# Asking for the raw rotary blocks of the first two-map head at the attention's begin

## The chip, the cores and the metric

One core of a Trainium2 chip runs the whole kernel. The metric is the device time of one execution in microseconds. The kernel before took 2370.1 us, the median of three runs (2368.41 to 2372.17). Its engines are TensorE (PE in the profile, with PEld for its weight loads), VectorE (DVE), ScalarE (ACT), GpSimd (POOL) and SyncE (SP). Each has its own queue of instructions and runs it in order. Transfers (DMAs) are issued from the queues of SP, ACT and POOL.

## The reference

Two layers of an encoder run over 512 tokens of width 1024 in float32. Each layer is a half-step feed-forward network, a mixer and a second half-step feed-forward network. The mixer is what the change touches:

```
u = rmsnorm(h);  proj = u @ w_in
qa, ka, va, qb, kb, vb, qc, kc, vc, gl = split(proj)
oa = neighbourhood_attention(qa, ka, va, rpb)            # 8 heads, A
ob = sliding_window_attention(rope(qb), rope(kb), vb, sink)   # 8 heads on 2, B
oc = differential_attention(rope(qc), rope(kc), vc, lam)  # 4 heads, two maps each, C
gates = sigmoid(gl + b_gate)                              # one per branch
merged = sum_n gates[n] * (branch[n] @ w_branch[n])
h = h + rmsnorm(merged @ w_out)

def apply_rope(t, cos, sin):
    t1, t2 = split(t, 2)
    return t * cos + concat(-t2, t1) * sin
```

## The kernel before

Activations lie with the features on the 128 partitions and 512 tokens along the row. A float32 product is made from split operands: a value is taken apart into a high part (on ACT) and the rest (on DVE), and three matmuls add up high by high, high by low and low by high. `mm3` does this in lines 326 to 328, and `dense1` calls it for one output block of 128 features over all the input blocks. Its weights come from DRAM in 512 KB pieces (`fetch`, tile wr, mostly from ACT's queue in this stage) and are split by `ensure` (L224 on ACT, L225 on DVE).

A layer projects first. The project stage computes queries, keys and values of all three branches, and POOL stores many of them to DRAM: split halves (tile part) and the unrotated query and key blocks of branch C (tile raw, eight in a layer, L1405). Then the mixer stage begins. A string, ORDER, lists its units in the order in which the program writes them:

```
qa0 qa1 aa0 gb0 gb1 qa2 aa1 ga0 qa3 aa2 ga1 kb qb0 aa3 ga2 ga3 qb1 ab0 ...
... qb3 ab2 gb6 gb7 qc0 ab3 ga4 ga5 qc1 ac0 ...
```

A unit qa loads what one pair of heads of branch A needs: stacked queries and keys (`restacked`, tile st, two DMAs of 64 rows each, L1783 and L1784), values (`values`, tile x from part, L1760) and the raw relative-position bias (braw, L1729). A unit aa does that pair's attention: scores on TensorE (L1675), the maximum with the bias added (L1678), exponentials on ACT, the reciprocal of the sum (L1692), then in `rest` a transpose (L1706), a split (`split`, L352 and L353) and the product with the values (L1709 and L1710). Units ga, gb and gc are the gates, dense matmuls on TensorE that wait for nothing but weights. A unit kb loads the rotary tables cosR and sinR (`tables_in`, L1943). A unit qc loads one head of branch C: `qkv_c` calls `rope` for its query and its key block. `rope` issues from SP the raw block (x, L1760) and four DMAs of 32 rows that load the same block with its halves swapped (sh, L1768), and then lets DVE multiply x by cosR (L1769), sh by sinR (L1770) and add them (L1771).

The order in which the program writes these units is not the order on the engines. In the mixer, up to its output product, a scheduler places every instruction on its engine's queue, by the order of the program as priority and by its own model of times. It also places the buffers: the tag tx has five slots (x and sh of `rope`), st has fourteen. So DVE's first rotary product of branch C stands in the middle of branch A's second and third pair, and dense matmuls of the gates are spread between the scores and the value products. The DMAs on SP are placed in the same way, and one waits on SP's queue until its buffer and its source are free, and for the landing of earlier transfers; those behind it wait with it. Lines 1760, 1768 to 1771, 1783, 1784 and 1943 are the ones to follow.

Of the kernel before, what the change touches and what calls it, by code (L numbers as in the profile page):

```python
# [39 lines left out]
QA, KA, VA, QB, KB, VB, QC, KC, VC, GL = 0, 4, 8, 12, 16, 17, 18, 22, 26, 30  # L40
# [79 lines left out]
def encoder_kernel(ctx: ExitStack, tc: tile.TileContext, order, xT, wts, cols, rows, rpb, consts, tables, out):  # L120
# [30 lines left out]
    def big(tag, dt=F32, shape=(P, T), name="v"):  # L151
        if tag in BUFS:
            return sb.tile(list(shape), dt, tag=tag, name=nm(name), bufs=BUFS[tag])
        kind, pool = phase[0]
        return pool.tile(list(shape), dt, tag=tag, name=nm(name), bufs=ABUFS[kind][tag])
# [1482 lines left out]
    def raw_of(l, hd):  # L1638
        return bass.AP(rpb.tensor, (l * 8 + hd) * 16 * RPBW, [[RPBW, 8], [1, 16], [1, 8 * RPBW]])
# [77 lines left out]
    def mixer(l, op, made):  # L1717
# [6 lines left out]
        def ask(hd):  # L1724
            if hd < 2:
                raws[hd] = pre[:, 2 + hd, :]
                return
            raw = raws[hd] = big("g", name="braw")
            nc.sync.dma_start(raw, raw_of(l, hd))  # L1729
# [28 lines left out]
        def load(d, dt=F32, tag="tx"):  # L1758
            x = big(tag, dt, name="x")
            nc.sync.dma_start(f(x), d)  # L1760
            return x

        def rope(c):
            x = load(made[c])
            sh = big("tx", name="sh")
            for q in range(4):
                o = q ^ 1
                nc.sync.dma_start(sh[32 * q : 32 * q + 32], made[c][32 * o : 32 * o + 32])  # L1768
            V.tensor_tensor(out=x, in0=x, in1=turning[0], op=ALU.mult)  # L1769
            V.tensor_tensor(out=sh, in0=sh, in1=turning[1], op=ALU.mult)  # L1770
            V.tensor_tensor(out=x, in0=x, in1=sh, op=ALU.add)  # L1771
            return x

        def restacked(c, both):
            if c in (QA, KA):
                return made[c]
            hi, lo = made[c]
            res = []
            for s in range(2):
                own, pair_ = slice(64 * s, 64 * s + 64), []  # L1780
                for one, two in ((hi, lo), (lo, hi))[: 2 if both else 1]:
                    st = big("st", F32R, name="st")
                    nc.sync.dma_start(f(st)[0:64], one[own])  # L1783
                    nc.sync.dma_start(f(st)[64:128], two[own])  # L1784
                    pair_.append(st)
                res.append((pair_ + [None])[:2])
            return res

        def values(c):
            t = made[c] if c == VA else [load(d, F32R, "st") for d in made[c]]  # L1790
            if c >= VC:
                return t
            v = [x.rearrange("p (b h d) -> p b h d", b=2, h=2) for x in t]
            return lambda j, s: v[j // 2][:, j % 2, s, :]
# [13 lines left out]
        def qkv_a(p):  # L1808
            got = restacked(QA + p, False), restacked(KA + p, True), values(VA + p)
            for s in range(2):  # L1810
                ask(2 * p + s)
            return got

        oa = [sb.tile([P, 4, T], F32R, tag="X", name=nm("oa"), bufs=BUFS["X"]) for _ in range(2)]
# [131 lines left out]
        def qkv_c(hd):  # L1946
            return stacks(rope(QC + hd), False), stacks(rope(KC + hd), True), values(VC + hd)
# [19 lines left out]
        def do(u):  # L1967
            kind, i = u[:2], int(u[2:] or 0)
            if kind == "fc" or kind[0] == "y":
                if kind == "fc" and i >= len(oc) or kind[0] == "y" and (kind[1], 3) not in OT:  # L1970
                    settle()
            if kind == "qa":
                held[u] = qkv_a(i)
            elif kind == "kb":
                tables_in()
                held["kb"] = qkv_b(KB), values(VB)
            elif kind == "qb":
                held[u] = qkv_b(QB + i)
            elif kind == "qc":
                held[u] = qkv_c(i)  # L1980
            elif kind == "aa":
                attn_a(i, *held.pop(f"qa{i}"))
            elif kind == "ab":
                attn_b(i, held.pop(f"qb{i}"), *held["kb"])
            elif kind == "ac":
                attn_c(*held.pop(f"qc{i}"))
            elif kind == "fc":
                finish_c(i)
            elif kind[0] == "g":
                gates("abc".index(kind[1]), i)  # L1990
            elif kind[0] == "y":
                combine("abc".index(kind[1]), kind[1], i)
# [146 lines left out]
```

## Time and profile before

| what | value |
| --- | --- |
| median of three runs | 2370.1 us (2368.41 to 2372.17) |
| the profiled execution's own time | 2370.88 us |
| its span | 2369.1 us |
| TensorE busy | 2342.6 us, 99% |
| VectorE busy | 1892.4 us, 80% |
| ScalarE busy | 1446.8 us, 61% |
| mean granted TensorE clock | 0.996 |

The profile is of one execution. Times in it count from the start of the span. A line of a timeline gives the start, the duration, the engine, the line of the program, the operation with the tile that it writes and those that it reads, and, in brackets, how long the engine was idle before it and what released it. A line of waits gives the waiting operation, what it waited for, the microseconds in all, the number of times and the longest. A line of DMA issues gives the transfer, the queue, the count, the size and the median of the time from issue to landing. The mixer of the first layer begins near 516 us, and that of the second near 1688 us.

### The profile page before, as it was taken

What the parts mean: (1) busy time and instruction counts of PE and PEld (TensorE: products, weight loads), DVE (VectorE), ACT (ScalarE), POOL (GpSimd) and SP (SyncE); (2) the same over time, 40 slices, a digit from 0 to 9 for tenths busy, and PEclk for the clock granted to TensorE, in tenths of its full rate; (3) what the DMA queues carried; (4) which work ended last, traced back from release to release, by engine and by line L of the source; (5) the groups of instructions that cost most, each with busy time, mean ns of one, the idle gap of its engine ahead of it and who ended that gap; (6) DMA issues with size and microseconds to landing.
All of it is one profiled execution on the core that took longest, in us unless ns stands there. A gap on an engine that the chain in (4) does not pass through costs nothing. (4 is left out here: it accounts for less than half of the span.)

```text
span 2369.1 us, 40269 instructions
## 1 busy us (share of the span) xinstructions
PE 2342.6 (99%) x15134; PEld 2109.5 (89%) x15134; DVE 1892.4 (80%) x3082; ACT 1446.8 (61%) x2715; POOL 223.8 (9%) x354
## 2 busy tenths in 40 slices
PE   9999999999999999999999999999999999999998
PEld 8999889997888889998899998889978788899987
DVE  7887988966888668888878878889579876788796
ACT  6555566667777465655655554666687764556563
POOL 0111001110121001110001110011101200011100
PEclk9999999999999999999999999999999999999999
DMA  5566446667565524664525565276774664256642
GB/s 170 162 169 190 154 145 187 207 219 207 168 174 189 167 97 147 166 162 165 175 87 168 162 178 196 102 216 199 222 206 139 195 206 140 97 147 172 190 148 84
DMA packets 138147, 395.16 MB, mean 167 GB/s; under 512 B 19296, under 2 KB 26080, under 8 KB 137440
## 3 DMA queue, kind: packets, MB, share of 16 engines
q1 hardware_dynamic: 102960, 260.37, 35.0%
q0 software_dynamic: 20160, 78.66, 12.4%
q10 hardware_dynamic: 14832, 53.56, 7.4%
q8 instruction: 119, 1.95, 0.3%
q14 instruction: 76, 0.62, 0.1%
HBM read 326.98 MB, written 80.74 MB: 172 GB/s over the span
## 5 line engine op out<-in xcount | busy, mean ns | idle before, releaser
L680 PE MATMUL mm<-X,h 128*128 128x256 f32 x1504 | 268.0, 278 | 1.2 <-DVE v L738 1.2
L680 PEld LDWEIGHTS mm<-X,h 128*128 128x128 f32 x1504 | 228.5, 188 | 2.5 <-DVE v L738 2.0
L225 DVE TENSOR_TENSOR w<-wr,w 128x512 fp32r<-128x512 f32 x264 | 178.9, 685 | 56.2 <-ACT w L224 55.2
L224 ACT ACTIVATE w<-wr 128x512 fp32r<-128x512 f32 x264 | 162.5, 627 | 96.4 <-PE mm L328 40.8
L326 PE MATMUL mm<-X,w 128*128 128x512 f32 (+1 forms) x570 | 218.3, 383 | 1.8 <-ACT X L553 1.8
L328 PE MATMUL mm<-X,w 128*128 128x512 f32 (+1 forms) x570 | 216.4, 380 | 0.8 <-DVE w L225 0.8
L327 PE MATMUL mm<-X,w 128*128 128x512 f32 (+1 forms) x570 | 216.2, 379 | 0.8 <-DVE X L554 0.7
L680 PE MATMUL mm<-ht,h 128*128 128x256 f32 x752 | 210.1, 279 | 0.0
L680 PE MATMUL mm<-ht,l 128*128 128x256 f32 x752 | 210.1, 279 | 0.0
L680 PE MATMUL mm<-lt,h 128*128 128x256 f32 x752 | 209.4, 278 | 0.0
L680 PE MATMUL mx<-ht,h 128*128 128x256 f32 x752 | 208.3, 277 | 0.6 <-ACT v L724 0.6
L680 PE MATMUL mm<-X,l 128*128 128x256 f32 x752 | 208.2, 277 | 0.0
L680 PE MATMUL mx<-ht,l 128*128 128x256 f32 x752 | 208.1, 277 | 0.0
L680 PE MATMUL mx<-lt,h 128*128 128x256 f32 x752 | 207.9, 277 | 0.0
L630 DVE TENSOR_TENSOR l<-wr,h 128x1024 fp32r<-128x1024 f32 x94 | 114.9, 1222 | 65.7 <-PE mm L680 65.7
L662 ACT ACTIVATE h<-wr 128x1024 fp32r<-128x1024 f32 x94 | 99.9, 1062 | 78.7 <-PE mx L680 55.5
L680 PE MATMUL at<-X,w 128*128 128x256 f32 x1128 | 144.2, 277 | 0.0
L680 PEld LDWEIGHTS mx<-ht,h 128*128 128x128 f32 x752 | 141.2, 188 | 1.4 <-ACT v L724 1.4
L680 PEld LDWEIGHTS mm<-ht,l 128*128 128x128 f32 x752 | 141.7, 188 | 0.1
L680 PEld LDWEIGHTS mm<-ht,h 128*128 128x128 f32 x752 | 141.7, 188 | 0.0
L680 PEld LDWEIGHTS mm<-lt,h 128*128 128x128 f32 x752 | 141.7, 188 | 0.0
L680 PEld LDWEIGHTS mx<-ht,l 128*128 128x128 f32 x752 | 141.2, 188 | 0.2 <-DVE l L640 0.2
(458 smaller groups left out, 6802.4 us busy)
## 6 DMA issues: line engine op xcount, KB each, us to landing
wr<-in_wts_dram SPq DMA_DIRECT2D x273, 512.0 KB, 4.6
wr<-in_wts_dram ACTq DMA_DIRECT2D x102, 512.0 KB, 4.1
sum<-in_wts_dram POOLq DMA_DIRECT2D x64, 512.0 KB, 5.3
st<-part SPq DMA_DIRECT2D x120, 128.0 KB, 5.1
ap<-in_wts_dram SPq DMA_DIRECT2D x20, 512.0 KB, 5.6
a<-kept SPq DMA_DIRECT2D x32, 256.0 KB, 6.3
ap<-sum SPq DMA_DIRECT2D x16, 512.0 KB, 4.3
x<-part SPq DMA_DIRECT2D x32, 256.0 KB, 3.8
```

The lines of the kernel that those rows point to most:

```text
L224: A.activation(hi, raw, AF.Copy)
L225: V.tensor_tensor(out=lo, in0=raw, in1=f(hi), op=ALU.subtract)
L326: PE.matmul(acc, w[0], x[0], start=start, stop=False)
L327: PE.matmul(acc, w[0], x[1], start=False, stop=False)
L328: PE.matmul(acc, w[1], x[0], start=False, stop=stop)
L630: V.tensor_tensor(out=w["l1"], in0=self.raws[g][0], in1=f(w["h1"]), op=ALU.subtract)
L662: A.activation(self.W[g]["h24"], self.raws[g][1], AF.Copy)
L680: PE.matmul(acc, ws[i], xs[j], start=start and k == m == 0, stop=stop and k == n - 1 and m == 2, skip_group_check=True,)
```

## The change

A new function `begun(c)` holds the five DMAs that `rope` used to issue itself. `qkv_a(0)`, the loads of branch A's first pair, now calls it for QC and KC, the query and key blocks of branch C's first head, after its own loads in the program. `rope` takes those two from a dictionary and issues the DMAs itself for the other three heads. Both layers have the change. Lines behind it move: in the listings below L1769, L1770 and L1771 become L1775, L1776 and L1777, L1783 and L1784 become L1789 and L1790, and L1943 becomes L1952.

```diff
--- before.py
+++ after.py
@@ -1760,12 +1760,18 @@
             nc.sync.dma_start(f(x), d)
             return x
 
-        def rope(c):
+        def begun(c):
             x = load(made[c])
             sh = big("tx", name="sh")
             for q in range(4):
                 o = q ^ 1
                 nc.sync.dma_start(sh[32 * q : 32 * q + 32], made[c][32 * o : 32 * o + 32])
+            return x, sh
+
+        raws_c = {}
+
+        def rope(c):
+            x, sh = raws_c.pop(c, None) or begun(c)
             V.tensor_tensor(out=x, in0=x, in1=turning[0], op=ALU.mult)
             V.tensor_tensor(out=sh, in0=sh, in1=turning[1], op=ALU.mult)
             V.tensor_tensor(out=x, in0=x, in1=sh, op=ALU.add)
@@ -1809,6 +1815,9 @@
             got = restacked(QA + p, False), restacked(KA + p, True), values(VA + p)
             for s in range(2):
                 ask(2 * p + s)
+            if p == 0:
+                for c in (QC, KC):
+                    raws_c[c] = begun(c)
             return got
 
         oa = [sb.tile([P, 4, T], F32R, tag="X", name=nm("oa"), bufs=BUFS["X"]) for _ in range(2)]
```

The scheduler places everything anew. Three places of the first layer show it; the second layer has the same pattern. The first is SP's queue where the mixer begins, and where the tables stand. In the kernel before, x_7488 is the raw query block, and its swapped pieces are sh_7490:

```order
L211 DMA wr_5748<-in_wts_dram 128x1024
L1783 DMA st_5920<-part_4051 64x512
L1784 DMA st_5920<-part_4053 64x512
...
L1729 DMA braw_6147<-in_rpb_dram 128x1x512
L1729 DMA braw_6149<-in_rpb_dram 128x1x512
L1943 DMA cosR_6548<-in_tables_dram 128x512
L1943 DMA sinR_6550<-in_tables_dram 128x512
L1760 DMA x_7488<-raw_5146 128x512
...
L1729 DMA braw_6359<-in_rpb_dram 128x1x512
L1729 DMA braw_6361<-in_rpb_dram 128x1x512
L1768 DMA sh_7490<-raw_5146 32x512 x4
```

In the changed kernel x_5920 and sh_5922 are of the query block, x_5927 and sh_5929 of the key block:

```order
L211 DMA wr_5748<-in_wts_dram 128x1024
L1760 DMA x_5920<-raw_5146 128x512
L1768 DMA sh_5922<-raw_5146 32x512 x4
L1760 DMA x_5927<-raw_5151 128x512
L1768 DMA sh_5929<-raw_5151 32x512 x4
L1789 DMA st_5934<-part_4051 64x512
L1790 DMA st_5934<-part_4053 64x512
...
L1729 DMA braw_6161<-in_rpb_dram 128x1x512
L1729 DMA braw_6163<-in_rpb_dram 128x1x512
L1952 DMA cosR_6562<-in_tables_dram 128x512
L1952 DMA sinR_6564<-in_tables_dram 128x512
L1760 DMA x_6157<-part_4631 128x512
L1760 DMA x_6159<-part_4633 128x512
```

The ten DMAs moved from behind the tables and further back to a place ahead of the first st; the tables kept their place among the others.

The second place is DVE's queue around the first rotary product. Before:

```order
L1678 ISA s_6235,nmx_6234<-mx_6248,bedge_6228 128x256
L1678 ISA nmx_6234 128x1
L225 TENSOR_TENSOR w_6762<-wr_6760,w_6762 128x512
L1769 TENSOR_TENSOR x_7488<-x_7488,cosR_6548 128x512
L1692 RECIPROCAL l_6252<-l_6252 128x4
L353 TENSOR_TENSOR lo_6267<-at_6263,hi_6266 128x256
L1744 TENSOR_TENSOR bedge_6364<-braw_6147,pre_5225 128x256
L353 TENSOR_TENSOR lo_6276<-at_6272,hi_6275 128x256
L1744 TENSOR_TENSOR bmid_6365<-braw_6147,pre_5225 128x256
```

In the changed kernel:

```order
L1678 ISA s_6249,nmx_6248<-mx_6262,bedge_6242 128x256
L1678 ISA nmx_6248 128x1
L1775 TENSOR_TENSOR x_5920<-x_5920,cosR_6562 128x512
L1776 TENSOR_TENSOR sh_5922<-sh_5922,sinR_6564 128x512
L1775 TENSOR_TENSOR x_5927<-x_5927,cosR_6562 128x512
L1777 TENSOR_TENSOR x_5920<-x_5920,sh_5922 128x512
L1692 RECIPROCAL l_6266<-l_6266 128x4
L353 TENSOR_TENSOR lo_6281<-at_6277,hi_6280 128x256
L1776 TENSOR_TENSOR sh_5929<-sh_5929,sinR_6564 128x512
L1777 TENSOR_TENSOR x_5927<-x_5927,sh_5929 128x512
L353 TENSOR_TENSOR lo_6290<-at_6286,hi_6289 128x256
```

Before, one rotary operation stood ahead of the reciprocal and of L353, and the other five further back. Now four stand ahead of the reciprocal and two behind the first L353.

The third place is TensorE's queue at the first scores of branch A's second pair (mx from st). Before:

```order
L328 MATMUL mm_6088<-X_3648,w_6069 128x512
L1710 MATMUL o_6011<-lo_6025,early_3957 128x256
L1675 MATMUL mx_6160<-st_5926,st_5920 128x256
L1709 MATMUL o_6011<-hi_6033,early_3957 128x256
L1675 MATMUL mx_6160<-st_5929,st_5920 128x256
L1675 MATMUL mx_6164<-st_5926,st_5920 128x256
L1675 MATMUL mx_6164<-st_5929,st_5920 128x256
L1706 MATMUL at_6187<-cons,s_5984 128x128 x2
L326 MATMUL mm_6302<-X_3646,w_6091 128x512
L1710 MATMUL o_6011<-lo_6034,early_3957 128x256
```

In the changed kernel:

```order
L327 MATMUL mm_6316<-X_3647,w_6105 128x512
L328 MATMUL mm_6316<-X_3646,w_6105 128x512
L326 MATMUL mm_6316<-X_3648,w_6120 128x512
L327 MATMUL mm_6316<-X_3649,w_6120 128x512
L328 MATMUL mm_6316<-X_3648,w_6120 128x512
L1675 MATMUL mx_6174<-st_5940,st_5934 128x256
L1675 MATMUL mx_6178<-st_5940,st_5934 128x256
L1709 MATMUL o_6200<-hi_6204,early_3957 128x2x128
L1710 MATMUL o_6200<-lo_6205,early_3957 128x2x128
...
L328 MATMUL mm_6316<-X_3648,w_6120 128x512
L326 MATMUL mm_6316<-X_3648,w_6120 128x512
L1675 MATMUL mx_6174<-st_5943,st_5934 128x256
L1675 MATMUL mx_6178<-st_5943,st_5934 128x256
L327 MATMUL mm_6316<-X_3649,w_6120 128x512
L1709 MATMUL o_6200<-hi_6222,early_3957 128x256
```

The first two of those scores moved behind fifteen more dense gate matmuls, the next two behind nineteen. Further on, 103 dense matmuls of the mixer stood ahead of the second half of these scores before, and 137 do now; ahead of the pair's first product with its values (the first L1710 that reads a loaded x) it was 123 and is 157. When branch B's first scores begin both kernels have 260.

## The prediction

> **What bounds the kernel now.** I read the page's busy table and the waits of TensorE first, then the timeline of PE, DVE and SP around the one large wait, and last the busy time by stage.
>
> ```profile
> PE 2342.6 (99%) x15134; PEld 2109.5 (89%) x15134; DVE 1892.4 (80%) x3082; ACT 1446.8 (61%) x2715; POOL 223.8 (9%) x354
> ...
> PE o L1710 <- DVE lo L353: 6.9, 2, 3.7
> ```
>
> TensorE is busy 99% of the span, so a change that leaves its instructions alone can win only its idle time and whatever lowers its clock. The largest idle entry is 6.9 us in two waits, one per layer, of the value matmul L1710 for DVE's L353. This is the first layer's:
>
> ```profile
> 553.45 0.29 PE L1709 MATMUL o<-hi,x 128*128 128x256 f32 x1
> 553.57 0.39 PE L327 MATMUL mm<-X,w 128*128 128x512 f32 x1
> 553.80 0.40 PE L328 MATMUL mm<-X,w 128*128 128x512 f32 x1
> 557.87 0.58 PE L1710 MATMUL o<-lo,x 128*128 128x256 f32 x1 [3.67 <-DVE lo L353]
> 558.53 0.78 PE L326 MATMUL mm<-X,w 128*128 128x512 f32 x1
> 563.36 0.40 PE L328 MATMUL mm<-X,w 128*128 128x512 f32 x1
> ```
> ```profile
> 550.44 0.68 DVE L225 TENSOR_TENSOR w<-wr,w 128x512 fp32r<-128x512 f32 x1
> 556.73 0.69 DVE L1769 TENSOR_TENSOR x<-x,cosR 128x512 f32<-128x512 f32 x1 [5.60 <-DMA x<-raw]
> 557.34 0.17 DVE L1692 RECIPROCAL l<-l 128x4 f32<-128x4 f32 x1
> 557.43 0.39 DVE L353 TENSOR_TENSOR lo<-at,hi 128x256 fp32r<-128x256 f32 x1
> ```
> ```profile
> 1729.85 0.39 PE L1710 MATMUL o<-lo,x 128*128 128x256 f32 x1 [3.21 <-DVE lo L353]
> 1730.80 0.63 PE L328 MATMUL mm<-X,w 128*128 128x512 f32 x1
> 1733.79 0.55 PE L326 MATMUL mm<-X,w 128*128 128x512 f32 x1
> ```
>
> DVE is idle for 5.60 us in front of the first rotary product, which waits for the raw query block; the split L353 that TensorE needs stands behind it in DVE's queue and has nothing to do with the rotary. From the start of that product to TensorE's restart it is 557.87 − 556.73 = 1.14 us. TensorE ran dry at 557.87 − 3.67 = 554.20, so DVE may come to the product as late as 554.20 − 1.14 = 553.06 before TensorE suffers; it was ready at 551.05 (550.44 + 0.61, the step from 556.73 to 557.34). Its slack is 2.0 us.
>
> The idle time has a tail:
>
> ```profile
> 544.00:552.00 8.00, 8.00 (x46) 6.90 (x46) 6.39 (x28) 6.45 (x20) 0.00 (x0) 1.00 0.92 238
> 552.00:556.00 4.00, 2.20 (x10) 1.37 (x9) 0.00 (x0) 1.30 (x6) 0.00 (x0) 1.00 1.06 278
> 556.00:560.00 4.00, 2.13 (x7) 1.84 (x8) 1.88 (x6) 2.46 (x7) 0.00 (x0) 0.56 0.92 217
> 560.00:564.00 4.00, 4.00 (x13) 3.15 (x12) 1.12 (x4) 0.97 (x4) 0.00 (x0) 0.58 0.88 208
> 564.00:590.00 26.00, 25.53 (x156) 21.98 (x155) 23.77 (x80) 25.00 (x74) 0.54 (x1) 1.00 0.60 174
> 590.00:605.00 15.00, 15.00 (x84) 12.62 (x84) 10.83 (x35) 10.42 (x31) 0.62 (x1) 1.00 0.72 213
> ```
>
> The columns are the stretch, its length, the busy time of PE, PEld, DVE, ACT and POOL, then TensorE's granted clock and the DMA share. After the idle the clock is 0.56 and 0.58. From 558.53 to 563.36 there are eleven steps of dense matmuls in 4.83 us; at the 0.23 us of 553.57 to 553.80 they would take 2.53, so 2.3 us are lost. In the second layer seven steps take 2.99 us instead of 1.61: 1.4 lost. The two waits together cost 6.9 + 2.3 + 1.4 = 10.6 us. That bounds what this change can win.
>
> A shorter wait has no such tail:
>
> ```profile
> 11.55 0.38 PE L326 MATMUL mx<-X,w 128*128 128x256 f32 x1 [2.09 <-ACT w L224]
> ...
> 8.00:12.00 4.00, 1.91 (x15) 1.71 (x15) 2.54 (x7) 2.34 (x7) 0.00 (x0) 1.00 1.01 386
> 12.00:16.00 4.00, 4.00 (x36) 4.00 (x35) 3.97 (x9) 3.81 (x10) 0.00 (x0) 1.00 0.79 265
> ```
>
> Idle of 2.09 us left the clock at 1.00, 3.21 us did not. The Trainium skill, "TensorE: Matmul & The Clock Gate", Part 1: The HAM clock gate, says the same with a figure: the clock halves after an idle window of about 3.4 us, and the window runs free, so a wait near that length is halved or not by its phase. By that rule a left-over wait of 1 us costs 1 us and no more, and one a little over 3 us might bring 0 or some 2 us of tail; the sum below needs only the two rows.
>
> **What goes.** The raw query block now lands long before 550, so the 5.60 us on DVE lose the releaser they are put down to. All of the 10.6 us would go if nothing else were late.
>
> **What is late next: the tables.** The products also need cosR and sinR, and these keep their place on SP's queue, behind the ten new issues:
>
> ```profile
> 495.75 1.07 SPq L1784 DMA_DIRECT2D st<-part  x1
> 516.27 0.44 SPq L1783 DMA_DIRECT2D st<-part  x1
> ...
> 546.81 0.45 SPq L1943 DMA_DIRECT2D cosR<-in_tables_dram  x1
> 547.69 0.33 SPq L1943 DMA_DIRECT2D sinR<-in_tables_dram  x1
> 548.06 0.43 SPq L1760 DMA_DIRECT2D x<-raw  x1
> ...
> 561.43 2.30 SPq L1768 DMA_DIRECT2D sh<-raw  x4
> ```
> ```profile
> st<-part SPq DMA_DIRECT2D x10, 128.0 KB, 5.0
> ...
> cosR<-in_tables_dram SPq DMA_DIRECT2D x1, 256.0 KB, 7.4
> ```
>
> Already in the kernel before, cosR landed at 546.81 + 7.4 = 554.2 and sinR at about 555.1, after the 553.06 at which TensorE begins to suffer; the raw block came just behind them. With everything else in place, taking the raw block away would give back only 556.7 − 554.2 = 2.5 us of DVE's wait. So it matters where both sides now stand.
>
> SP's side: one load and its four swapped pieces take 0.43 + 2.30 = 2.73 us of issue, two sets 5.5 us. Low end of the delay to the tables: none, if the ten fit into the 19.5 us in which SP stood between 496.8 and 516.27. High end: 5.5 us. I take the high end, because SP also waits for landings between its issues and the new ten push every later one back by ten places in that sequence. cosR is then issued at 552.3 and sinR at 553.2, landing (7.4 us) at 559.7 and 560.6.
>
> TensorE's and DVE's side: by the printed order, 123 of the mixer's dense gate matmuls (L326 to L328) stand ahead of the stalled L1710 before and 157 after. The 34 more take 34 × 0.23 = 7.8 us, so TensorE runs dry at 554.20 + 7.8 = 562.0, not 554.2. On DVE four rotary operations instead of one now stand ahead of the reciprocal and L353. From sinR's landing there are three operations (0.61 us each) and the 1.14 − 0.61 = 0.53 us to the restart: 2.36 us. The restart is at 560.6 + 2.36 = 563.0: **TensorE waits 1.0 us**, in each layer, at full clock. Ends of this term: 0 (tables undelayed; the three added operations just fit into the 2.0 us of slack) and 2.1 (sinR 1.1 us later, still no tail).
>
> **What the moved matmuls cost where they left.** The 34 dense matmuls were fillers between softmax steps. The order has both kernels level again, at 260 dense matmuls, when the sliding window's scores begin, near 605. In 564 to 590 ACT is busy 25.00 of 26 us: ACT sets the pace there and dense matmuls only fill TensorE.
>
> ```profile
> L225 DVE TENSOR_TENSOR w<-wr,w 128x512 fp32r<-128x512 f32 x264 | 178.9, 685 | 56.2 <-ACT w L224 55.2
> L224 ACT ACTIVATE w<-wr 128x512 fp32r<-128x512 f32 x264 | 162.5, 627 | 96.4 <-PE mm L328 40.8
> ```
>
> With 34 matmuls go three weight splits (a split weight block serves twelve): 3 × 0.627 = 1.9 us of ACT and 2.1 us of DVE. TensorE's work in the stretch falls by 7.8 us, ACT's by 1.9. Behind it, in 590 to 605, ACT has 15 − 10.42 = 4.6 us free. New idle time of TensorE per layer: at most 7.8 − 1.9 = 5.9 us, if nothing of the 4.6 can be used; at least 5.9 − 4.6 = 1.3. I take **1.7 us**, near the low end: in 590 to 605 it is TensorE's fillers (15.00 of 15) that hold ACT back, so softmax work moves up when they are fewer; and five of the six rotary operations of DVE (3.4 us) leave the tight stretch as well.
>
> **What costs nothing.** The rotary's arithmetic is the same six operations. The second pair's stacked blocks stand behind the new loads on SP:
>
> ```profile
> L1675 PE MATMUL mx<-st,st x28: 276/280/365, 531.2 to 568.8; 128*128 128x256 f32 x28
> ```
>
> Issued up to 5.5 us after 516 to 520 and landing 5.0 us later, they are there by about 531; their first use moves from 531.2 behind fifteen dense matmuls, to 534.6. The cover is 3 us; beyond it TensorE would wait by the difference.
>
> **Sum.** −10.6 + 2 × 1.0 + 2 × 1.7 = −5.2 us. The profiled execution took 2370.88 (span 2369.1 and 1.8 around it), 0.8 over the median of the runs: 2365.7 on its own scale, **2364.9** as a median.
>
> **Rivals.**
> *The tables take the raw block's place in full.* sinR lands 2.2 us later than worked out (562.8), TensorE waits 3.2 us again and the clock drops again. For it: the DMA share of 0.92 to 1.06 from 544 to 560, when the tables travel, and 7.4 us for 256 KB. Against it: 0.5 MB of raw loads leave just this stretch. It gives back 10.6 us, and with some shortage of fillers 2370 to 2372: no change that can be told.
> *Slower: TensorE starves in the softmax stretch.* The place is 564 to 605, where 34 fillers are missing. If ACT cannot pull up work, 5.9 us of idle per layer: −10.6 + 2.0 + 11.8 = +3.2, 2373; if the idle comes in pieces of over 3 us the tail of 1.4 to 2.3 is paid again and it is 2376 to 2377. It decides from (10.6 − 2.0) / 2 = 4.3 us per layer on. For it: ACT at 25.00 of 26. Against it: the 4.6 us free behind.
> *All of it is won.* The tables are not delayed, TensorE's later need covers them, and the fillers aren't missed: 2370.1 − 10.6 = 2359.5. For it: 7.8 us of cover against at most 5.5 of delay. Against it: the tight stretch.
>
> **How the numbers follow.** Forecast 0.50, with a range of its own of 2361 to 2368; tables 0.24; starving 0.14; all won 0.12. A difference under 0.2% (4.7 us: 2365.4 to 2374.8) cannot be told from none here. The forecast's range lies 4.4 of its 7 us below 2365.4, so 0.33 of its 0.50 is faster; with all won and a little of the rest, faster is 0.47. Slower by over 0.2% needs the tail in the starving case or both rivals together: 0.13. The rest, 0.40, is the same. The range of 8 in 10 reaches from all won to starving without tail: 2359.3 to 2373.
>
> **What would show it.** In the changed kernel: DVE's idle before the rotary product put down to cosR or sinR (or gone), no longer to x<-raw; L1710's wait under 2.1 us in both layers and the granted clock 1.00 in the 8 us behind it; cosR issued near 552; and in the 40 us after it TensorE idle by 1 to 3 us more per layer, waiting for DVE or ACT. The prediction is wrong if a wait of 3 us or more stands at that L1710 or at the second pair's first scores, if the clock drops elsewhere, or if idle of over 4 us gathers in the softmax stretch.

## The result

The changed kernel takes 2382.6 us (median of six runs, 2380.2 to 2383.5) against 2369.3 us before (six runs). The ratio is 1.0061, with a 95% interval of 1.0050 to 1.0071: 0.6% slower, some 14 us, where 2364.9 was forecast and 2373 was the upper end of the range.

The changed kernel's busy table, and then its waits of TensorE:

```profile
PE 2343.7 (98%) x15134; PEld 2109.4 (89%) x15134; DVE 1896.1 (80%) x3082; ACT 1448.0 (61%) x2715; POOL 222.8 (9%) x354
```
```profile
PE o L1710 <- DVE lo L353: 13.1, 2, 7.1
PE o L1709 <- ACT hi L352: 3.8, 2, 1.9
...
PE mx L1675 <- DVE nmx L1678: 2.1, 2, 1.1
```

The span grew from 2369.1 to 2381.5, by 12.4 us. TensorE's idle time grew from 2369.1 − 2342.6 = 26.5 to 2381.5 − 2343.7 = 37.8, by 11.3; the other 1.1 us are longer busy time. The wait that was to shrink from 6.9 to 2.0 us grew to 13.1, and two new ones stand beside it. It is the same L1710 in both layers. TensorE's timeline of the changed kernel around it:

```profile
562.85 0.40 PE L326 MATMUL mm<-X,w 128*128 128x512 f32 x1
570.32 0.58 PE L1710 MATMUL o<-lo,x 128*128 128x256 f32 x1 [7.07 <-DVE lo L353]
...
1750.62 0.58 PE L1710 MATMUL o<-lo,x 128*128 128x256 f32 x1 [6.07 <-DVE lo L353]
```

and DVE's:

```profile
567.11 0.69 DVE L1775 TENSOR_TENSOR x<-x,cosR 128x512 f32<-128x512 f32 x1 [7.16 <-DMA cosR<-in_tables_dram]
567.97 0.69 DVE L1776 TENSOR_TENSOR sh<-sh,sinR 128x512 f32<-128x512 f32 x1 [0.16 <-DMA sinR<-in_tables_dram]
568.57 0.69 DVE L1775 TENSOR_TENSOR x<-x,cosR 128x512 f32<-128x512 f32 x1
569.18 0.69 DVE L1777 TENSOR_TENSOR x<-x,sh 128x512 f32<-128x512 f32 x1
569.78 0.17 DVE L1692 RECIPROCAL l<-l 128x4 f32<-128x4 f32 x1
569.87 0.39 DVE L353 TENSOR_TENSOR lo<-at,hi 128x256 fp32r<-128x256 f32 x1
```

DVE no longer waits for the raw block. It waits for the tables, which land 13 us later than before: cosR at 567.1 instead of about 554.2. SP's timeline shows how they came to be so late:

```profile
494.94 1.44 SPq L1760 DMA_DIRECT2D x<-raw  x1
507.78 1.73 SPq L1768 DMA_DIRECT2D sh<-raw  x4
510.64 0.34 SPq L1760 DMA_DIRECT2D x<-raw  x1
512.41 10.40 SPq L1768 DMA_DIRECT2D sh<-raw  x4
522.92 0.49 SPq L1789 DMA_DIRECT2D st<-part  x1
...
536.19 0.44 SPq L1790 DMA_DIRECT2D st<-part  x1
...
551.85 0.45 SPq L1789 DMA_DIRECT2D st<-part  x1
...
556.90 0.62 SPq L1952 DMA_DIRECT2D cosR<-in_tables_dram  x1
557.56 0.48 SPq L1952 DMA_DIRECT2D sinR<-in_tables_dram  x1
```

and SP's waits between 480 and 580 name what it stood for:

```profile
SPq L1768 <- PE mx L680: 11.4, 1, 11.4
SPq L1768 <- DMA wr<-in_wts_dram: 10.3, 2, 8.9
...
SPq L1790 <- DMA wr<-in_wts_dram: 6.3, 1, 6.3
SPq L1789 <- DMA wr<-in_wts_dram: 5.2, 1, 5.2
```

In the kernel before, over the same window:

```profile
SPq L1783 <- DMA part<-lo: 19.3, 1, 19.3
...
SPq L1784 <- DMA wr<-in_wts_dram: 10.1, 2, 7.1
```

The first raw block goes out at 494.9. Its swapped pieces wait 11.4 us, until 507.8, for a matmul of the projection (L680). The last pieces of the key block wait 8.9 us for the landing of a weight load. So the ten entries hold the queue from 494.9 to 522.8. Before, the first st block (two entries) had gone out at 495.2, SP had then stood 19.3 us until one of the projection's stores (part) had landed, and the rest followed from 516.3. Now the first st goes out at 522.9, the twelfth of these entries at 536.2 instead of 524.7, and cosR at 556.9 instead of 546.8. From the first of these entries to cosR, SP waits 38.5 us instead of 32.3 by its rows of waits; the other 4 us of the delay are issue time. Then it takes 10.2 us to land (556.9 to 567.1), not 7.4.

By stage of 10 us (columns as in the windows of before: the stretch, its length, PE, PEld, DVE, ACT, POOL, the granted clock, the DMA share):

```profile
560.00:570.00 10.00, 3.24 (x19) 2.46 (x17) 2.73 (x6) 2.50 (x10) 0.00 (x0) 0.91 0.89 216
570.00:580.00 10.00, 9.69 (x44) 8.32 (x45) 7.47 (x23) 6.55 (x18) 0.06 (x1) 0.74 0.51 139
590.00:600.00 10.00, 8.76 (x57) 7.35 (x55) 6.82 (x25) 9.84 (x31) 0.00 (x0) 1.00 0.54 157
```

The largest part of the loss is the one wait with its slowed tail (560 to 580): 6.2 of the 11.3 us of new idle time are the growth of the wait at L1710. A smaller second one lies near 600, where ACT is busy 9.84 of 10 us and TensorE waits for its L352 (3.8 us in both layers).

### The profile page after: what moved, and what is told of

Its sections match the earlier page's. It is cut to its first block, busy times and chain, and to the rows that moved or that the text cites. A ratio compares the mean times of both kernels' runs of the same rounds, so it can differ in the third digit from the quotient of the medians.

```text
span 2381.5 us, 40264 instructions
## 1 busy us (share of the span) xinstructions
PE 2343.7 (98%) x15134; PEld 2109.4 (89%) x15134; DVE 1896.1 (80%) x3082; ACT 1448.0 (61%) x2715; POOL 222.8 (9%) x354
## 3 DMA queue, kind: packets, MB, share of 16 engines
q0 software_dynamic: 20160, 78.66, 12.4%
## 5 line engine op out<-in xcount | busy, mean ns | idle before, releaser
L680 PE MATMUL mm<-X,h 128*128 128x256 f32 x1504 | 268.1, 278 | 2.0 <-DVE v L738 2.0
L225 DVE TENSOR_TENSOR w<-wr,w 128x512 fp32r<-128x512 f32 x264 | 179.2, 686 | 74.5 <-ACT w L224 73.4
L680 PEld LDWEIGHTS mm<-X,h 128*128 128x128 f32 x1504 | 228.4, 188 | 3.4 <-DVE v L738 2.7
L680 PE MATMUL mm<-ht,h 128*128 128x256 f32 x752 | 210.2, 280 | 0.0
L680 PE MATMUL mm<-ht,l 128*128 128x256 f32 x752 | 210.0, 279 | 0.0
L680 PE MATMUL mm<-lt,h 128*128 128x256 f32 x752 | 209.4, 278 | 0.0
L680 PE MATMUL mx<-ht,h 128*128 128x256 f32 x752 | 208.5, 277 | 0.3 <-ACT v L724 0.2
L680 PE MATMUL mm<-X,l 128*128 128x256 f32 x752 | 208.2, 277 | 0.0
L680 PE MATMUL mx<-ht,l 128*128 128x256 f32 x752 | 208.1, 277 | 0.1
L680 PE MATMUL mx<-lt,h 128*128 128x256 f32 x752 | 207.9, 277 | 0.0
L680 PE MATMUL at<-X,w 128*128 128x256 f32 x1128 | 144.1, 277 | 0.0
L680 PEld LDWEIGHTS mx<-ht,h 128*128 128x128 f32 x752 | 141.2, 188 | 0.8 <-ACT v L724 0.7
L680 PEld LDWEIGHTS mm<-lt,h 128*128 128x128 f32 x752 | 141.7, 188 | 0.0
L680 PEld LDWEIGHTS mm<-ht,h 128*128 128x128 f32 x752 | 141.7, 188 | 0.0
L680 PEld LDWEIGHTS mm<-ht,l 128*128 128x128 f32 x752 | 141.7, 188 | 0.0
L680 PEld LDWEIGHTS mx<-ht,l 128*128 128x128 f32 x752 | 141.2, 188 | 0.3 <-DVE l L640 0.3
```

Of the source, the lines that this page charges most:

```text
L225: V.tensor_tensor(out=lo, in0=raw, in1=f(hi), op=ALU.subtract)
L680: PE.matmul(acc, ws[i], xs[j], start=start and k == m == 0, stop=stop and k == n - 1 and m == 2, skip_group_check=True,)
```

## The experiments

Three theories were put to the test. The *queue theory*: the ten transfers ahead on SP's queue, with the waits that they bring, push everything behind them back, and the wait of DVE moves from the raw block to the tables. The *order theory*: the loss lies in what the scheduler did with TensorE and DVE (34 fillers pulled ahead, four rotary operations ahead of L353), wherever the transfers stand. The *bandwidth theory*: the early traffic slows the tables' transfer.

### The same ten transfers from POOL's queue

```diff
-        def begun(c):
+        def begun(c, eng=nc.sync):
...
-                    raws_c[c] = begun(c)
+                    raws_c[c] = begun(c, nc.gpsimd)
```

> The ten raw DMAs at the same place of the program, but issued from POOL's queue; SP's queue is the old one without its raw entries, and TensorE has 123 dense matmuls ahead of the first L1710 with a loaded x, as before. Queue theory (the ten entries on SP push the tables back): cosR is issued within 1 us of 546.8 and lands near 554.2, DVE's wait before the rotary product is put down to cosR or sinR and lasts 3 to 4.5 us, L1710's wait falls from 3.7 and 3.2 to 1.5 to 3 us, and the time is 2362 to 2370. Order theory (the moved dense matmuls and the four rotary operations ahead of L353 cost, wherever the DMAs stand): with the old order of TensorE the time is that of before, 2366 to 2372, and cosR's issue says nothing. Bandwidth theory (more early traffic slows the tables): cosR takes 9 us or more to land although it is issued at its old time.

Measured: 2375.3 us, ratio 1.0034 (1.0020 to 1.0049). Slower than before, though not as slow as the changed kernel. The lines of SP, DVE and ACT:

```profile
548.97 0.72 SPq L1953 DMA_DIRECT2D cosR<-in_tables_dram  x1
```
```profile
558.09 0.69 DVE L1776 TENSOR_TENSOR x<-x,cosR 128x512 f32<-128x512 f32 x1 [3.23 <-DMA cosR<-in_tables_dram]
```
```profile
545.43 0.36 ACTq L211 DMA_DIRECT2D wr<-in_wts_dram  x1
545.89 0.63 ACT L224 ACTIVATE w<-wr 128x512 fp32r<-128x512 f32 x1 [4.68 <-DMA st<-part]
```

cosR goes out 2.2 us late, not within 1 as the queue theory said, and takes 9.1 us to land; L1710 waits 3.06 and 4.56 us, where 1.5 to 3 were expected. But the larger new loss is one that no theory had: ACT stands 4.68 us in front of its own weight load, until an st block that SP had asked for has landed; DVE's L225 and TensorE's scores wait behind it (a wait of 3.05 us at L1675, and 1.90 in the second layer). So a late transfer of SP also stops ACT, which computes nothing in that time. The 9.1 us of landing are what the bandwidth theory said; the times of the other two (2362 to 2370, 2366 to 2372) were missed.

### The ten transfers behind the second pair's loads

```diff
-            if p == 0:
+            if p == 1:
                 for c in (QC, KC):
                     raws_c[c] = begun(c)
```

> The ten raw DMAs written behind the second pair's loads instead of the first pair's: on SP they stand behind the first twelve st entries, two x and two braw, still ahead of the tables. TensorE's order is that of the changed kernel (137 dense ahead of the second half of the second pair's scores, 157 ahead of the first L1710 with a loaded x). Queue theory: the tables are still behind all ten, cosR is issued near 553 to 558, L1710 waits 4 to 7 us, 2376 to 2383. Order theory: 2380 to 2384, as the changed kernel, with the same wait. Buffer theory (what costs is the wait for buffers at the head of SP's queue, 11 us for a TensorE release, before any st is asked for): the st entries go out at 516 again, cosR near 550, and the time falls to 2368 to 2374.

Measured: 2373.1 us, ratio 1.0020 (1.0008 to 1.0031). This is the cleanest pair of the study: from the second half of the second pair's scores on, TensorE has the changed kernel's counts (137, 157, 176 ... 260), DVE has its four rotary operations ahead of the reciprocal, and the ten transfers are still early. Only the place on SP's queue differs, behind sixteen entries instead of ahead of them. SP and DVE:

```profile
527.14 0.44 SPq L1760 DMA_DIRECT2D x<-raw  x1
...
553.19 0.46 SPq L1952 DMA_DIRECT2D cosR<-in_tables_dram  x1
```
```profile
563.31 0.69 DVE L1775 TENSOR_TENSOR x<-x,cosR 128x512 f32<-128x512 f32 x1 [5.68 <-DMA cosR<-in_tables_dram]
```

cosR goes out 3.7 us sooner than in the changed kernel and lands 3.8 us sooner. The L1710 waits are 5.5 and 3.2 instead of 7.1 and 6.1, and of the ratio's 0.61% two thirds are gone (0.41%, 9.7 us). The time is that of the third expected way (2368 to 2374), by which the wait at the head of SP's queue costs before any st is asked for; the st entries do go out at 515.5 again. The issue of cosR and the waits are those of the queue theory, which had 553 to 558 for the one and 2376 to 2383 for the time. The order theory's 2380 to 2384 falls as the whole explanation. cosR is still issued 6.4 us later than before, and the kernel is still slower than before.

### The raw query block alone

```diff
+            if p == 0:
+                raws_c[QC] = load(made[QC])
...
-            x, sh = raws_c.pop(c, None) or begun(c)
+            x, sh = begun(c, raws_c.pop(c, None))
```

> Only the raw query block itself is asked for at the attention's begin, one DMA; its four swapped pieces and the key block stay where they were. TensorE's order is nearly that of before (105 and 124 dense). Queue theory: one more entry ahead delays the tables by 0 to 2 us; DVE's wait ends at cosR's landing, 554 to 556 instead of 556.7; the L1710 wait falls to 1 to 3 us per layer and the clock stays up in at least one layer: 2360 to 2368. Order theory: same order, so the same time as before within 3 us. Tables theory (cosR is as late as the raw block was, whatever is moved): no change, wait put down to cosR, 2367 to 2372.

Measured: 2386.6 us, ratio 1.0081 (1.0066 to 1.0096), outside all three. TensorE's timeline:

```profile
555.56 0.39 PE L1710 MATMUL o<-lo,x 128*128 128x256 f32 x1 [1.06 <-DVE lo L353]
...
584.32 0.77 PE L1675 MATMUL mx<-st,st 128*128 128x256 f32 x2 [5.74 <-DMA st<-part]
```

At the place in question it did what the queue theory said: the wait of 3.67 us shrank to 1.06 (to 2.61 in the second layer), since one entry hardly delays cosR. But the scheduler placed the later work anew as well: from 572 to 584 not one dense matmul stands between the scores and value products on TensorE, and the st block that the next scores need lands 5.7 us too late. The gain at one place was lost thirty microseconds on, where a late transfer met a stretch without fillers.

### The tables early too

```diff
             if p == 0:
                 for c in (QC, KC):
                     raws_c[c] = begun(c)
+                tables_in()
...
             elif kind == "kb":
-                tables_in()
```

> Raw blocks as in the changed kernel, and the two table loads right behind them, ahead of the first st: twelve DMAs early, none of them late. TensorE has even more dense matmuls ahead (144 and 165). Queue theory: nothing that the rotary products need is late, the L1710 wait for DVE's L353 is under 1 us in both layers, and with the fillers missing later the time is 2360 to 2370. Order theory: 42 dense matmuls ahead instead of 34 cost as much as in the changed kernel or more, 2378 to 2386. If st of the second pair now comes too late, a wait of TensorE at L1675 for a DMA appears instead.

Measured: 2383.2 us, ratio 1.0061 (1.0043 to 1.0079). The first head's rotary products now run at 531.9 without a wait. DVE's next wait:

```profile
566.34 0.69 DVE L1775 TENSOR_TENSOR x<-x,cosR 128x512 f32<-128x512 f32 x1 [4.79 <-DMA x<-raw]
```

It is the raw block of the second head (issued at 557.5), which the scheduler moved into the gap, again ahead of an L353 that TensorE needs (2.75 and 1.33 us). The queue theory's 2360 to 2370 missed: with the first late block out of the way, the next late one stood in the same place. But that is not the whole loss. The waits at L1710 are 4.9 us in all, 2 less than in the kernel before. The largest are now at L1675, for DVE's maximum (5.6 us), and L1706 waits 3.4 us for ACT; neither is among the rows of waits of the kernel before. The order theory's 2378 to 2386 holds the measured time. Whether missing fillers or late transfers made these waits is not shown.

### The rotary held back, nothing asked for early

Here the kernel before gets an order of its own on DVE. `ended[p]` is the last DVE instruction of pair p (the split of its result, L1828), and `issue_after` only places the block's instructions behind it on their engine.

```diff
-            V.tensor_tensor(out=x, in0=x, in1=turning[0], op=ALU.mult)
-            V.tensor_tensor(out=sh, in0=sh, in1=turning[1], op=ALU.mult)
-            V.tensor_tensor(out=x, in0=x, in1=sh, op=ALU.add)
+            with tc.issue_after(ended[2].ins):
+                V.tensor_tensor(out=x, in0=x, in1=turning[0], op=ALU.mult)
+                V.tensor_tensor(out=sh, in0=sh, in1=turning[1], op=ALU.mult)
+                V.tensor_tensor(out=x, in0=x, in1=sh, op=ALU.add)
```

> The kernel before, with branch C's rotary arithmetic ordered on DVE behind the end of branch A's third pair. SP's queue and TensorE's order up to branch B are those of before, entry for entry. Head-of-queue theory (the price of a late raw block or table is only that a rotary product stands in DVE's queue ahead of L353): DVE's wait for x<-raw is gone, L1710's waits of 3.7 and 3.2 us fall below 0.7, the clock stays at 1.00 in the stretch behind, and 7 to 11 us are won: 2358 to 2362. Rival (the DMAs of this stretch are the limit, and the next thing asked of them is late instead): another wait of 2 us or more, for st or braw, takes the place, and the time is 2365 to 2372.

Measured: 2363.4 us, ratio 0.9978 (0.9968 to 0.9989). Faster than both kernels, by 0.22% or some 5 us (3 to 8) against the kernel before; 7 to 11 us and 2358 to 2362 were expected. cosR and the raw block go out when they did before (546.6 and 548.2); only DVE doesn't stand in front of them. In place of the 3.67 us:

```profile
557.96 0.38 PE L1709 MATMUL o<-hi,x 128*128 128x256 f32 x1 [1.06 <-ACT hi L352]
```

What is left of the wait comes by way of ACT. In the kernel before, ACT's next weight load is issued only at 556.66, as the raw block lands, and here ACT stands before that load until the same block has landed:

```profile
556.66 0.34 ACTq L211 DMA_DIRECT2D wr<-in_wts_dram  x1
```
```profile
555.55 0.34 ACTq L211 DMA_DIRECT2D wr<-in_wts_dram  x1
555.93 1.71 ACT L1695 ACTIVATE s<-s,l 128x256 f32<-128x256 f32 x4 [3.03 <-DMA x<-raw]
```

So it seems that two engines stood for the raw block in the kernel before, and holding the rotary frees only DVE.

A variant holds it behind pair 1 instead (`ended[1]`):

> The kernel before with the rotary arithmetic ordered on DVE behind the end of branch A's second pair instead of the third. It then stands behind the four L353 that TensorE waits for, and its data landed at 556.7, so nothing should wait: no wait of L1710 over 0.7 us, the clock at 1.00 behind it, and 2358 to 2365. If holding it for one pair is not enough (the pair ends before the raw block's swapped pieces have landed at about 568), DVE waits for sh<-raw and some 1 to 3 us per layer come back: 2363 to 2369.

Measured: 2361.7 us, ratio 0.9974 (0.9959 to 0.9990). Its windows over the place of the old wait:

```profile
552.00:560.00 8.00, 7.86 (x42) 6.22 (x42) 3.67 (x14) 5.73 (x17) 0.00 (x0) 1.00 1.03 245
560.00:568.00 8.00, 8.00 (x50) 6.87 (x49) 7.16 (x28) 7.66 (x25) 0.00 (x0) 1.00 0.70 186
```

TensorE is busy 15.86 of 16 us and the clock is 1.00. Its profiled span is 2358.9 against 2369.1: 10.2 us, close to the 10.6 that the two waits and their tails were worked out at. By the runs it is 0.26%, 6 us (2 to 10), inside the 2358 to 2365 that were expected. So it was DVE's order that was to be changed. Its price is near 10 us only in the profiled executions (9.2 us of span with `ended[2]`, 10.2 with `ended[1]`); the runs of both variants put it at 5 to 6, and 10.6 lies outside both intervals. ACT still stands 2.11 us for the raw block here.

### The changed kernel with the rotary held

The changed kernel with the same four lines (`ended[2]`):

> The changed kernel with the same order on DVE: raw DMAs early, tables late at 556.9, TensorE's 137 and 156 dense matmuls ahead as in the changed kernel, but no rotary product ahead of L353. Head-of-queue theory: the L1710 waits of 7.1 and 6.1 us fall below 1, with their clock loss some 9 to 10 us per layer at most; the time falls by 14 to 20 us to 2363 to 2369, though the tables still land at 567. Order theory (the moved fillers and the late st blocks cost by themselves): 4 us or more of other waits stay in each layer between 555 and 610, and the time stays above 2372.

Measured: 2394.1 us, ratio 1.0105 (1.0088 to 1.0122). The wait of L1710 is gone, and the kernel is slower still. ACT's and TensorE's timelines:

```profile
571.89 0.33 ACTq L211 DMA_DIRECT2D wr<-in_wts_dram  x1
572.27 0.59 ACT L1712 ACTIVATE ot<-o 64x512 f32<-64x512 f32 x1 [5.99 <-DMA st<-part]
```
```profile
574.31 0.39 PE L1709 MATMUL o<-hi,x 128*128 128x256 f32 x1 [4.34 <-DVE nmx L1678]
```

As with the transfers from POOL, ACT stands in front of a weight load until a late st block has landed, here for 5.99 us, and then TensorE waits 4.34 us for what ACT had still to do. (The row puts the wait down to DVE's maximum; the weight load of the same L1709 waits 4.77 us for ACT's L352.) The tables were the first late transfer to be met; behind them the st blocks were late too. The head-of-queue theory's 2363 to 2369 missed; of the order theory's expectation the sign and the 4 us of other waits came true, though the largest of them came from a transfer. Another 7.4 us, in six waits of 1.9 and less at L1709 for ACT's L352, are not put down to one.

The same two edits together, with the ten transfers behind the second pair's loads:

> Both orders together: the ten raw DMAs behind the second pair's loads on SP, and the rotary arithmetic held behind branch A's third pair on DVE. TensorE's and DVE's orders in the second and third pair are those of e6; only the place of the ten DMAs on SP differs (ahead of the first st there, behind sixteen entries here). Queue theory (late transfers cost in whatever stands behind them, also at the st blocks and at ACT's weight loads): the 4.3 and 4.1 us waits at L1709 of e6 fall to under 2, and the time falls by 10 us or more to 2368 to 2382. Order theory (the 33 dense matmuls that were pulled ahead and the later rotary starve TensorE, wherever the DMAs stand): the waits at L1709 stay within 1 us of e6 and the time is 2388 to 2396.

Measured: 2385.3 us, ratio 1.0074 (1.0049 to 1.0099). The 4.34 us became 0.57:

```profile
570.81 0.39 PE L1709 MATMUL o<-hi,x 128*128 128x256 f32 x1 [0.57 <-DVE nmx L1678]
```

The place on SP's queue is worth 0.31% here (some 7 us; the two intervals overlap a little) with the same orders of TensorE and DVE in these pairs, after 0.41% in the first pair of kernels. The queue theory's wait came true, its time (2368 to 2382) was missed by 3 us; the order theory's 2388 to 2396 was missed too. What is left, 1.0074 against 0.9978 for the same rotary order on the kernel before, is the fillers' new place together with ten transfers still ahead of the tables and the third pair. These two were not taken apart. The waits at L1709 for ACT's L352 are still 7.3 us (2.1 with the rotary held on the kernel before), and one at L1675 for an st block is 2.1.

### Half of the change: the query block alone, with its pieces

```diff
             if p == 0:
-                for c in (QC, KC):
-                    raws_c[c] = begun(c)
+                raws_c[QC] = begun(QC)
```

> Half of the change: only the query block's five DMAs are asked for at the attention's begin, the key block's stay where they were. TensorE has 119 and 140 dense matmuls ahead. Queue theory: the delay of the tables is smaller than with ten entries, cosR is issued near 550 to 554, DVE's wait is put down to cosR, L1710 waits 3 to 5 us per layer, 2370 to 2377. If the delay comes from the wait of the first entries for their buffers and not from their number, cosR is as late as with ten (556 to 557) and the time 2378 to 2384.

Measured: 2380.4 us, ratio 1.0050 (1.0035 to 1.0065). SP and TensorE:

```profile
551.50 0.68 SPq L1951 DMA_DIRECT2D cosR<-in_tables_dram  x1
```
```profile
564.10 0.58 PE L1710 MATMUL o<-lo,x 128*128 128x256 f32 x1 [5.30 <-DVE lo L353]
```

With five entries ahead the tables go out 4.7 us late, with ten 10.1: the delay grows with their number. That is the first expected way; the time is 3 us over its range and inside that of the second (2378 to 2384), whose late cosR did not come. The first had left something out: with half of the change only 17 dense matmuls (140 − 123) stand between the wait and its old place, so TensorE runs dry at 558.8 and not at 563.3. The tables land 6 us sooner than with ten, and the waits of 5.30 and 4.95 us are not much shorter.

## Why the prediction was wrong

**The bound.** Right in its mechanism: the wait at L1710 came from a rotary product at the head of DVE's queue, and with that product held it is gone. The 10.6 us are borne out by the profiled executions of the two kernels that hold it (9.2 and 10.2 us less span); their runs give 5 to 6. That ACT too seems to have stood for the raw block was overlooked.

**What goes.** Right: the raw block is waited for no longer at that place.

**The tables' delay.** This is the step that failed. Its bounds were 0 and 5.5 us, the issue time of ten entries. It was 10.1 us (546.81 to 556.90). An entry's cost in SP's queue is not its issue time: the new entries brought waits of their own to the head of the queue (11.4 us for matmuls of the projection, 8.9 for a weight's landing). They lasted beyond the 19.3 us in which SP had stood before, so the third st entry went out at 524.3 instead of 516.3. The two waits for weights behind them (6.3 and 5.2) are not new: before they were 3.0 and 7.1. The prediction named such waits and then bounded the term without them. Moving the same ten entries behind sixteen others gave back 0.41%. Through this delay and the longer landing, L1710 waited 13.1 us where the sum had 2.0. That is 11.1 of the 17.6 us by which the profiled span (12.4 longer) missed the sum (5.2 shorter). The tail that the sum counted as won was paid again: the clock was 0.74 from 570 to 580.

**The tables' landing.** 7.4 us were taken from the row of before; it took 10.2 for cosR and 10.4 for sinR. Where DVE waited for cosR in the other kernels it was 6.3 to 10.1. That the early traffic is the reason is not shown: the transfers of the second pair's loads had moved into the same stretch.

**DVE and TensorE.** The arithmetic held. From sinR's landing to the restart it took 570.32 − 567.97 = 2.35 us (2.36 worked out), and TensorE ran dry at 563.25 (562.0). The wait of 7.07 instead of 1.0 is the 4.4 us by which sinR was issued later than taken, plus 3.0 of landing, less 1.25 of later need, and the forecast's own 1.0: 7.1.

**The fillers.** About right in idle time: 1.88 us in one wait near 600 against 1.7, for ACT as expected. Its slowed tail was not in the sum.

**What costs nothing.** The first scores of the second pair did not wait for their st blocks. The second half waited 0.96 and 1.15 us for DVE's maximum.

**The rivals.** The one that came true, the tables in the raw block's place, had a chance of 0.24 but a time of 2370 to 2372: it let the new wait grow to the size of the old one and no further, with the point of 562.8 taken as its end. (A slip without effect: 4.4 of 7 us is 0.31 of the 0.50 called faster, not 0.33.) A wait that moves to a later transfer is not bounded by the old wait. Of the signs to look for, x<-raw was to be replaced by cosR, and it was; cosR near 552 and a wait under 2.1 us were not.

## What to carry to other kernels

When an engine stands behind a transfer, look first at whether the waiting instruction can be placed behind the urgent work on its own queue: two kernels that only did this won 0.22% and 0.26%, while asking for the data earlier lost 0.61%. Look too for a second engine that stands for the same transfer. An early request costs what its own waits (for a buffer, for a landing) do to everything behind it in that queue, and the issue time is no upper bound for that; look up what will be at the head of the queue, and who needs the entries behind it. And where the next late thing is close (here tables 2.5 us ahead of the raw block), it inherits the wait; moving it too did not pay here, as the second head's block came next. What the fillers' new place cost by itself stays open.

## What the hardware showed beyond that

An engine that issues transfers between its computations can be stopped by another queue's transfer. ACT stood 4.68 us (from POOL's variant) and 5.99 us (changed kernel with the rotary held) in front of its own weight load until an st block of SP had landed, and 3.03 us for the raw block with the rotary held on the kernel before.

The clock's tail does not go by the length of a single wait alone. The prediction took 2.09 us as safe. In the changed kernel the same wait near the end of branch A lasted 1.88 us in the first layer and 1.89 in the second:

```profile
600.64 0.38 PE L1709 MATMUL o<-hi,x 128*128 128x256 f32 x1 [1.88 <-ACT hi L352]
...
1781.23 0.39 PE L1709 MATMUL o<-hi,x 128*128 128x256 f32 x1 [1.89 <-ACT hi L352]
```
```profile
600.00:604.00 4.00, 3.28 (x15) 2.79 (x16) 3.04 (x11) 3.99 (x11) 1.08 (x2) 0.80 0.58 201
604.00:608.00 4.00, 4.00 (x23) 3.75 (x22) 2.84 (x13) 2.15 (x8) 0.00 (x0) 0.77 0.89 258
...
1780.00:1784.00 4.00, 2.69 (x16) 2.29 (x17) 3.02 (x9) 3.99 (x10) 0.84 (x2) 1.00 0.77 238
```

The clock fell to 0.80 and 0.77 after the one and stayed at 1.00 after the other. The Trainium skill, "TensorE: Matmul & The Clock Gate", Part 1: The HAM clock gate, has a window that runs free of the program, with which two equal waits may differ as here; its idle time of about 3.4 us for the clock to fall does not hold for this row, where 1.88 us were enough.
